# Feed-forward of a two-layer encoder: two parts projected down together, twelve products to a bank

## The chip, the cores and the metric

The kernel runs on one core of one Trainium2 chip. A core has a matrix engine (TensorE, in the profile PE, with PEld for its weight loads), a vector engine (VectorE, DVE), an engine for activations and copies (ScalarE, ACT), a general one (GpSimd, POOL), and DMA queues that SyncE (SP) issues here. The engines run side by side, each through its own list of instructions in order, and wait for one another by semaphores. The metric is the device time of one execution in microseconds; lower is better.

## The reference

Two sequences of 1024 channels, a prompt of 256 tokens and a sample of 512, go through two layers and a last norm. Each layer is a mixer (an mLSTM in the first, attention in a window in the second) and a feed-forward with a convolution of width 3, both with a residual. The change lies in the feed-forward alone:

```python
def conv_ffn(h, w_up, conv_w, conv_b, w_down):
    u = h @ w_up                       # 1024 -> 2 * 2816
    u = lax.conv_general_dilated(u, conv_w[:, None, :], window_strides=(1,), ...) + conv_b
    g = u[..., :D_FF]
    val = u[..., D_FF:]
    return (jax.nn.silu(g) * val) @ w_down   # 2816 -> 1024

x = x + g2 * conv_ffn(h, ffn_w_up[l], ffn_conv_w[l], ffn_conv_b[l], ffn_w_down[l])
```

## The kernel before

**Columns and precision.** Prompt and sample stand side by side as 768 columns. A matrix product in fp32 is made of three in a shorter format: each operand is split into a high and a low half (`whi`, `wlo` for weights, `zh`, `zl` and the like for activations), and high·high, high·low and low·high are added in a PSUM bank. A split is a cast on ACT (L275, the high half) and a subtraction on DVE (L276, the low half). Raw weights come by DMA in pieces of 512 KB (`raw`, 5 buffers); the split weights have 3 buffers each.

**Parts.** `Net.ffn` works through the 2816 channels in `NPART` = 11 parts of 256. For a part p, `up(p)` projects 1024 channels to 256 gates and 256 values, convolves them, and forms silu(gate)·value; `down(p, g)` projects these 256 channels back to 1024 and adds into the residual slab `xt`. Written order: up(0), up(1), down(0), up(2), down(1), and so on to up(10), down(9), down(10). The framework's scheduler makes each engine's list out of this, so pieces of neighbouring steps interleave.

**A projection up.** `pair` (called for i = 0, the gates, and i = 1, the values) replaces eight quarter products by seven, with sums of weights and of activations. A quarter is 12 matmuls of 128x384 (L1350 high·high, L1351 high·low, L1353 low·high). The seven are called B11, B21, B22 and T1 to T4 after the activations that they read, and go to four banks that stay the same: a (B11, then B21), e (T1), b (T2 on top of a copy of B11, then B22), d (T3 on top of a copy of T2, then T4). In the listings with numbers these banks are `ps_4468` (a), `ps_4469` (e), `ps_4470` (b) and `ps_4471` (d). Between them stand copies on ACT: L1399 (a into b, before T2), L1404 (T1 out), L1410 (b into d, before T3), L1421 (T3 out, before T4 may write d), L1363 (a row out); and DVE's L1423 and L1424, which finish the rows. POOL makes the sums of raw weights (L1383, L1386, L1387, L1395). The convolution is L1587 on ACT and L1589, L1590 on DVE; the silu is L1597 on ACT.

**The product.** `product` multiplies gate and value on POOL (L1602, in two halves) and splits the result into a slab `g` (L275 and L276). Slabs are large buffers, 6 in all: 2 for `xt`, 2 for the rows of u, and 2 that `yrow` and `g` take in turn.

**A projection down.** `down` has two halves of weights, and in each 4 blocks of 128 output channels for the sample's 512 columns and the prompt's 256: 16 tiles. A tile is 6 matmuls (L269) into one bank of `pa` (4 banks); then `resid`, one instruction on DVE (L602), adds the bank, scaled, into `xt`. The last part, down(10), goes through ranges of 256 columns and runs the next norm behind them. Its code stays.

Of the kernel before, what the change touches and what calls it, by code (L numbers as in the profile page):

```python
# [12 lines left out]
R = mybir.dt.float32r  # L13
# [3 lines left out]
P = 128  # L17
# [7 lines left out]
RANGES = ((256, 512, 0), (512, 768, 0), PROMPT)  # L25
# [5 lines left out]
TG = T + GAP  # L31
# [3 lines left out]
NPART = FC // 2  # L35
# [45 lines left out]
def col(t):  # L81

    return t + (GAP if t >= 256 else 0)
# [7 lines left out]
class Norm:  # L91
# [31 lines left out]
    held = False  # L123
# [58 lines left out]
class Net:  # L182
# [1389 lines left out]
    def ffn(self, l, xt, pool, last_tile, apply, keep=None):  # L1572
        nc = self.nc
        u0 = U_FFN + l * NPART * 3
        early = self.prepare(u0)
        next(last_tile)

        urows = [self.slab([P, 4, TG]) for _ in range(2)]
        for urow in urows:
            nc.gpsimd.memset(urow[:, :, 256 : 256 + GAP], 0.0)  # L1580

        behind = []

        def conv(u, y, ch):
            cb = self.cst(CB + l * 44 + ch)
            w = lambda tap: self.cst(CW + (l * 44 + ch) * 3 + tap)
            nc.scalar.activation(y, u, AF.Identity, bias=cb, scale=w(1))  # L1587
            stt = nc.vector.scalar_tensor_tensor
            stt(y[:, 1:], u[:, :-1], w(0), y[:, 1:], ALU.mult, ALU.add)  # L1589
            stt(y[:, :-1], u[:, 1:], w(2), y[:, :-1], ALU.mult, ALU.add)  # L1590


        held = []

        def silu(yrow):
            for j in range(2):
                nc.scalar.activation(yrow[:, j], yrow[:, j], AF.Silu)  # L1597

        def product(yrow, g):
            for j in range(2):  # L1600
                y = yrow[:, 2 + j]
                nc.gpsimd.tensor_tensor(y, y, yrow[:, j], ALU.mult)  # L1602
                self.fp_copy_split(g[:, 0, j], g[:, 1, j], y)

        def up(p):
            urow = urows[0] if p == 0 else urows[1]
            fixed = lambda i: self.bank[i][:, :H]
            if p == 0:
                eng = mybir.EngineType
                self.ready(HALVES[0])  # L1610
                with self.tc.manual_schedule(engines={eng.PE, eng.Activation, eng.DVE}):
                    behind[:] = self.head(u0, last_tile, pool, urows, mark, early)
            yrow = self.slab([P, 4, TG])
            g = self.slab([P, 2, 2, TG], R)
            for i in range(2):
                if p:
                    rows = [urow[:, 2 * i + j] for j in range(2)]
                    with ExitStack() as order:
                        for ins in behind[2 * i :] if p == 1 else ():
                            order.enter_context(self.tc.issue_after(ins))  # L1620

                        other = p == i == 1
                        bank = lambda j: self.pa()[:, :H] if j == 1 and other else fixed(j)
                        self.pair(pool, u0 + 3 * p + i, bank, rows, p == 1, held.pop() if held else None)
                for j in range(2):
                    conv(urow[:, 2 * i + j], yrow[:, 2 * i + j], i * FC + 2 * p + j)
                if i == 0:
                    held.append(lambda: silu(yrow))
            if p:
                product(yrow, g)  # L1630
            else:
                gate = held.pop()
                held.append(lambda: (gate(), product(yrow, g)))
            return g

        def mark(t):

            hi, _ = self.quarter(self.B11)
            self.mm(t, hi[0][:, :P], hi[0], True, True)

        def down(p, g):
            ws = (w for _, w in self.halves(u0 + 3 * p + 2))
            chunk = lambda w, i: [t[:, 512 * i : 512 * (i + 1)] for t in w]

            def tile(w, c, rng, more=False):
                s0, s1, _ = rng
                alone = keep is None and p == NPART - 1
                o = (self.ps() if more and (c % 2 or alone) else self.pa())[:, : s1 - s0]
                cs = slice(c % 4 * P, (c % 4 + 1) * P)
                for i in range(2):  # L1650
                    wh, wl = chunk(w, i)
                    gh, gl = (g[:, z, i, col(s0) : col(s0) + s1 - s0] for z in range(2))
                    self.mm(o, wh[:, cs], gh, i == 0, False)
                    self.mm(o, wh[:, cs], gl, False, False)
                    self.mm(o, wl[:, cs], gh, False, i == 1)
                return self.resid(xt, o, l, 40, c, rng)

            if p < NPART - 1:
                for h, w in enumerate(ws):
                    for rng in SAMPLE, PROMPT:  # L1660
                        for c in range(4 * h, 4 * h + 4):
                            tile(w, c, rng, p == NPART - 2)
                return
            ws = list(ws)
            for rng in RANGES:
                final = keep is None and rng is RANGES[-1]
                norm = Norm(
                    self, xt, rng, apply, 3 if final else 4 if keep is None and rng is RANGES[1] else 2, final,
                    wait=0.0 if keep is None or rng is RANGES[-1] else 1.3,
                )  # L1670
                for c in range(KC):
                    done = tile(ws[c // 4], c, rng, keep is None or rng is not RANGES[-1])
                    norm.square(c)
                    if final and c >= KC - 2:
                        self.ends.append(done.ins)
                    if final and c == KC - 1:
                        norm.sums = [norm.sums[i] for i in (1, 2, 0, 3)]
                        norm.begin(1)
                    self.tick(0.65)
                if keep is not None:  # L1680
                    self.save_x(xt, keep, rng)
                self.start(rng, norm.stages())

        prev = None
        for p in range(NPART):
            g = up(p)
            if prev is not None:
                down(*prev)
            prev = (p, g)
        down(*prev)  # L1690


    def run(self):
# [178 lines left out]
```

## Time and profile before

| what | value |
|---|---|
| runs of the kernel | median 1809.89 us of 3, from 1808.83 to 1811.03 |
| the profiled execution | 1808.25 us |
| its span, first to last instruction | 1806.4 us |
| granted clock of TensorE, mean | 0.996 |
| feed-forward of the first layer | about 477 to 1015 us of the span |
| feed-forward of the second layer | about 1260 to 1806 us |

The profile is of one execution. Its rows name a line of the kernel, an engine, an operation and the buffers, written out<-in; "busy" is the time in which an engine works on something, "idle" the time ahead of an instruction, with what ended it behind the arrow. In a timeline the first number is the start, the second the duration. Matmuls overlap: one of 384 columns lasts 0.34 us in the rows while the next starts after some 0.17, so starts tell more than durations. Windows give the busy time of each engine in a stretch of the span.

### The profile page before, as it was taken

The page shows a single profiled execution, that of the slowest core. Times are in us where ns is not written, and L with a number is a line of the kernel's source. Part 1 is how long each engine was busy: PE and PEld are TensorE (multiplying, and loading weights), DVE is VectorE, ACT ScalarE, POOL GpSimd, SP SyncE. Part 2 cuts the span into 40 slices and gives each one's busy share as a digit, 9 for nine tenths or more (in the row PEclk, how much of TensorE's full clock was granted, in tenths as well). Part 3 has the DMA queues.
Part 4 walks back from the last instruction along what each step waited for, and adds up shares of the span by engine and source line. Part 5 has one row for each costly group of instructions (what it writes and reads, how often), then busy time and mean ns, then how long its engine had stood idle before and what let it go on. Part 6 is the DMA issues. An engine that isn't in the chain of part 4 may idle for free.

```text
span 1806.4 us, 28907 instructions
## 1 busy us (share of the span) xinstructions
PE 1773.1 (98%) x11206; PEld 1644.4 (91%) x11206; DVE 1384.8 (77%) x2219; ACT 887.8 (49%) x1789; POOL 488.2 (27%) x397
## 2 busy tenths in 40 slices
PE   7999999999999999999999999999999999999998
PEld 4988888889998999999999999889989999999997
DVE  4876777895799778777777867767998777777877
ACT  4544433444565444444444657665564444444443
POOL 3000000031024333333331313320144333333323
PEclk9999999999999999999999999999999999999999
DMA  9344665656212222222223331234122222222212
GB/s 360 98 140 135 196 207 180 215 180 219 71 59 71 62 67 71 70 71 71 67 64 94 106 93 42 60 92 138 48 82 71 71 71 71 70 70 71 70 36 71
DMA packets 64997, 185.08 MB, mean 102 GB/s; under 512 B 6247, under 2 KB 24839, under 8 KB 64732
## 3 DMA queue, kind: packets, MB, share of 16 engines
q1 hardware_dynamic: 64284, 182.72, 31.3%
q8 instruction: 88, 1.44, 0.3%
q10 hardware_dynamic: 576, 0.52, 0.1%
q14 instruction: 49, 0.40, 0.1%
HBM read 176.77 MB, written 6.44 MB: 101 GB/s over the span
## 4 chain that ended last, share of the span: by engine, by line
PE 87%; DVE 5%; DMA 3%; ACT 3%; issue 1%; POOL 1%; SPq 0%; DVEq 0%; ACTq 0%; POOLq 0%
PE ps L269 28%; PE pa L269 24%; PE ps L1350 11%; PE ps L1351 10%; PE ps L1353 10%; DMA raw<-in_adaln_t_dram 1%; PE pa L1189 1%; DVE junk L538 1%; DMA slab<-in_adaln_w_dram 1%; DVE wlo L276 1%; PE pa L1350 0%; PE pa L1351 0%; PE pa L1353 0%; ACT zh L1301 0%; DMA raw<-in_adaln_w_dram 0%
## 5 line engine op out<-in xcount | busy, mean ns | idle before, releaser
L275 ACT CAST whi<-raw 128x1024 fp32r<-128x1024 f32 (+1 forms) x231 | 241.0, 1045 | 339.0 <-PE pa L269 144.4
L276 DVE TENSOR_TENSOR wlo<-raw,whi 128x1024 fp32r<-128x1024 f32 (+1 forms) x231 | 312.6, 1354 | 119.1 <-ACT whi L275 116.8
L269 PE MATMUL pa<-slab,whi 128*128 128x256 f32 (+1 forms) x1280 | 307.6, 335 | 0.0
L269 PEld LDWEIGHTS pa<-slab,whi 128*128 128x128 f32 x1280 | 222.2, 188 | 21.6 <-DVE slab L602 0.4
L602 DVE SCALAR_TENSOR_TENSOR slab<-pa,mod,slab 128x256 f32<-128x256 f32 (+1 forms) x320 | 187.2, 603 | 62.7 <-PE pa L269 62.6
L269 PE MATMUL pa<-slab,wlo 128*128 128x512 f32 (+1 forms) x640 | 205.7, 334 | 0.0
L269 PE MATMUL ps<-zh,whi 128*128 128x256 f32 (+1 forms) x560 | 188.1, 337 | 0.3 <-ACT zh L948 0.3
L269 PE MATMUL ps<-zl,whi 128*128 128x256 f32 (+1 forms) x560 | 183.6, 330 | 0.5 <-DVE zl L563 0.5
L269 PE MATMUL ps<-zh,wlo 128*128 128x256 f32 (+1 forms) x560 | 181.7, 330 | 0.0
L1350 PE MATMUL ps<-zh,whi 128*128 128x384 f32 x504 | 172.6, 342 | 3.8 <-ACT nt L1421 2.0
L269 PE MATMUL ps<-slab,whi 128*128 128x384 f32 (+2 forms) x704 | 172.0, 329 | 0.9 <-DVE slab L276 0.5
L1351 PE MATMUL ps<-zl,whi 128*128 128x384 f32 x504 | 169.9, 337 | 0.8 <-DVE zl L1307 0.8
L1353 PE MATMUL ps<-zh,wlo 128*128 128x384 f32 x504 | 169.1, 336 | 0.0
L538 DVE CUSTOM_DVE_ANT_0 junk<-raw,crow,cstt 128x1024 f32<-128x1024 f32 x96 | 125.2, 1305 | 25.1 <-DMA raw<-in_adaln_t_dram 24.5
L1386 POOL TENSOR_TENSOR raw<-raw,raw 128x512 f32<-128x512 f32 x40 | 53.8, 1344 | 319.4 <-DVE wlo L276 246.3
L269 PEld LDWEIGHTS pa<-slab,wlo 128*128 128x128 f32 x640 | 120.4, 188 | 13.2 <-DVE wlo L276 0.4
L1602 POOL TENSOR_TENSOR slab<-slab 128x772 f32<-128x772 f32 x44 | 86.5, 1969 | 163.7 <-DVE slab L1590 150.5
L1589 DVE SCALAR_TENSOR_TENSOR slab<-slab,cstt,slab 128x771 f32<-128x771 f32 x88 | 105.4, 1200 | 26.5 <-ACT slab L1587 26.4
L269 PEld LDWEIGHTS ps<-slab,whi 128*128 128x128 f32 x704 | 122.5, 188 | 3.4 <-ACT whi L275 0.9
L269 PEld LDWEIGHTS ps<-zh,whi 128*128 128x128 f32 x560 | 106.8, 191 | 12.8 <-issue 3.5
L269 PEld LDWEIGHTS ps<-zl,whi 128*128 128x128 f32 x560 | 106.8, 191 | 9.5 <-DVE zl L563 0.7
L269 PE MATMUL ps<-slab,wlo 128*128 128x384 f32 (+2 forms) x352 | 114.8, 328 | 0.1
(301 smaller groups left out, 4286.8 us busy)
## 6 DMA issues: line engine op xcount, KB each, us to landing
raw<-in_w_dram SPq DMA_DIRECT2D x208, 512.0 KB, 3.7
raw<-in_adaln_t_dram SPq DMA_DIRECT2D x48, 512.0 KB, 4.2
raw<-in_adaln_w_dram SPq DMA_DIRECT2D x36, 512.0 KB, 4.5
slab<-in_x_dram SPq DMA_DIRECT2D x12, 512.0 KB, 7.2
slab<-in_adaln_w_dram SPq DMA_DIRECT2D x11, 512.0 KB, 9.2
slab<-mrows SPq DMA_DIRECT2D x8, 384.0 KB, 6.3
xs<-slab SPq DMA_DIRECT2D x6, 512.0 KB, 3.6
bt<-brow SPq DMA_DIRECT2D x16, 192.0 KB, 3.1
```

The source lines that it names most:

```text
L269: self.nc.tensor.matmul(out, lhsT, rhs, start=start, stop=stop)
L275: nc.scalar.copy(hi, src)
L276: return nc.vector.tensor_tensor(lo, src, hi.bitcast(F32), ALU.subtract)
L538: nc.vector.tensor_tensor_reduce(out=junk, in0=w, in1=row[:, s], scale=1.0, scalar=self.cst(AB + 48 * l + j), op0=ALU.mult, op1=ALU.add, a ...
L602: return self.nc.vector.scalar_tensor_tensor(x, o, self.mod[l][:, gc + c, q : q + 1], x, ALU.mult, ALU.add)
L1189: nc.tensor.transpose(pp[:, ks], b.t[:, e, ks], self.ident)
L1350: mm(o, wh[:, k], hi[k], start=start and k == 0, stop=False, skip_group_check=True)
L1351: mm(o, wh[:, k], lo[k], start=False, stop=False, skip_group_check=True)
L1353: mm(o, wl[:, k], hi[k], start=False, stop=k == 3, skip_group_check=True)
L1386: tt(q[0], q[2], q[0], ALU.subtract)
L1589: stt(y[:, 1:], u[:, :-1], w(0), y[:, 1:], ALU.mult, ALU.add)
L1602: nc.gpsimd.tensor_tensor(y, y, yrow[:, j], ALU.mult)
```

## The change

`down` takes two parts at once, (0, 1), (2, 3) and so on to (8, 9), and each of its 16 tiles now adds the six matmuls of the first part and the six of the second in one bank before `resid` takes it out. Both parts' first halves of weights are loaded, then both second halves. The order of the steps becomes up(0), up(1), up(2), down(0, 1), up(3), up(4), down(2, 3), to up(10), down(8, 9), down(10). The slabs `g` of two parts now have to live at once with a `yrow`. So `g` is taken only when the product is split, `yrow` only after the first `pair` is written, and the split of an even part from 2 on is held back: it is issued behind the copy L1410 (`fork`) of the next projection's first `pair`, through `behind`. An odd part's product is split at once.

```diff
@@ -1596,11 +1596,21 @@
             for j in range(2):
                 nc.scalar.activation(yrow[:, j], yrow[:, j], AF.Silu)
 
-        def product(yrow, g):
+        gs = {}
+
+        def product(yrow, p, now):
+            def part(j):
+                if not j:
+                    gs[p] = self.slab([P, 2, 2, TG], R)
+                self.fp_copy_split(gs[p][:, 0, j], gs[p][:, 1, j], yrow[:, 2 + j])
+
             for j in range(2):
                 y = yrow[:, 2 + j]
                 nc.gpsimd.tensor_tensor(y, y, yrow[:, j], ALU.mult)
-                self.fp_copy_split(g[:, 0, j], g[:, 1, j], y)
+                if now:
+                    part(j)
+            if not now:
+                held.append(lambda: [part(j) for j in range(2)])
 
         def up(p):
             urow = urows[0] if p == 0 else urows[1]
@@ -1610,8 +1620,7 @@
                 self.ready(HALVES[0])
                 with self.tc.manual_schedule(engines={eng.PE, eng.Activation, eng.DVE}):
                     behind[:] = self.head(u0, last_tile, pool, urows, mark, early)
-            yrow = self.slab([P, 4, TG])
-            g = self.slab([P, 2, 2, TG], R)
+            yrow = None
             for i in range(2):
                 if p:
                     rows = [urow[:, 2 * i + j] for j in range(2)]
@@ -1622,46 +1631,49 @@
                         other = p == i == 1
                         bank = lambda j: self.pa()[:, :H] if j == 1 and other else fixed(j)
                         self.pair(pool, u0 + 3 * p + i, bank, rows, p == 1, held.pop() if held else None)
+                yrow = yrow or self.slab([P, 4, TG])
                 for j in range(2):
                     conv(urow[:, 2 * i + j], yrow[:, 2 * i + j], i * FC + 2 * p + j)
                 if i == 0:
                     held.append(lambda: silu(yrow))
             if p:
-                product(yrow, g)
+                product(yrow, p, p % 2 == 1)
             else:
                 gate = held.pop()
-                held.append(lambda: (gate(), product(yrow, g)))
-            return g
+                held.append(lambda: (gate(), product(yrow, p, True)))
 
         def mark(t):
 
             hi, _ = self.quarter(self.B11)
             self.mm(t, hi[0][:, :P], hi[0], True, True)
 
-        def down(p, g):
-            ws = (w for _, w in self.halves(u0 + 3 * p + 2))
+        def down(parts):
+            of = [self.halves(u0 + 3 * p + 2) for p in parts]
+            g = [gs.pop(p) for p in parts]
             chunk = lambda w, i: [t[:, 512 * i : 512 * (i + 1)] for t in w]
 
-            def tile(w, c, rng, more=False):
+            def tile(ws, c, rng, more=False):
                 s0, s1, _ = rng
-                alone = keep is None and p == NPART - 1
+                alone = keep is None and len(parts) == 1
                 o = (self.ps() if more and (c % 2 or alone) else self.pa())[:, : s1 - s0]
                 cs = slice(c % 4 * P, (c % 4 + 1) * P)
-                for i in range(2):
+                steps = [(w, x, i) for w, x in zip(ws, g) for i in range(2)]
+                for w, x, i in steps:
                     wh, wl = chunk(w, i)
-                    gh, gl = (g[:, z, i, col(s0) : col(s0) + s1 - s0] for z in range(2))
-                    self.mm(o, wh[:, cs], gh, i == 0, False)
+                    gh, gl = (x[:, z, i, col(s0) : col(s0) + s1 - s0] for z in range(2))
+                    self.mm(o, wh[:, cs], gh, w is ws[0] and i == 0, False)
                     self.mm(o, wh[:, cs], gl, False, False)
-                    self.mm(o, wl[:, cs], gh, False, i == 1)
+                    self.mm(o, wl[:, cs], gh, False, w is ws[-1] and i == 1)
                 return self.resid(xt, o, l, 40, c, rng)
 
-            if p < NPART - 1:
-                for h, w in enumerate(ws):
+            if len(parts) == 2:
+                for h in range(2):
+                    ws = [next(x)[1] for x in of]
                     for rng in SAMPLE, PROMPT:
                         for c in range(4 * h, 4 * h + 4):
-                            tile(w, c, rng, p == NPART - 2)
+                            tile(ws, c, rng, parts[1] == NPART - 2)
                 return
-            ws = list(ws)
+            ws = [w for _, w in of[0]]
             for rng in RANGES:
                 final = keep is None and rng is RANGES[-1]
                 norm = Norm(
@@ -1669,7 +1681,7 @@
                     wait=0.0 if keep is None or rng is RANGES[-1] else 1.3,
                 )
                 for c in range(KC):
-                    done = tile(ws[c // 4], c, rng, keep is None or rng is not RANGES[-1])
+                    done = tile(ws[c // 4 : c // 4 + 1], c, rng, keep is None or rng is not RANGES[-1])
                     norm.square(c)
                     if final and c >= KC - 2:
                         self.ends.append(done.ins)
@@ -1681,13 +1693,12 @@
                     self.save_x(xt, keep, rng)
                 self.start(rng, norm.stages())
 
-        prev = None
         for p in range(NPART):
-            g = up(p)
-            if prev is not None:
-                down(*prev)
-            prev = (p, g)
-        down(*prev)
+            up(p)
+            if p > 1 and p % 2 == 0:
+                down((p - 2, p - 1))
+        held.pop()()
+        down((p,))
 
 
     def run(self):
```

Lines below the change stand 7 to 11 lines further down than in the profile of before.

**TensorE where up(1) ends and up(2) begins, first layer.** Of before; the first two rows are the end of T1 of up(2), `pa` are banks of down(0), and the last row is the first of T3 of up(1).

```order
L1351 MATMUL ps_4469<-zl,s1h_5870 128x384
L1353 MATMUL ps_4469<-zh,s1l_5871 128x384
L269 MATMUL pa_5723<-slab_5493,whi_5719 128x512 x2
L269 MATMUL pa_5731<-slab_5493,whi_5719 128x512 x2
L269 MATMUL pa_5739<-slab_5493,whi_5719 128x512 x2
L269 MATMUL pa_5723<-slab_5493,wlo_5720 128x512
L269 MATMUL pa_5723<-slab_5493,whi_5719 128x512
L269 MATMUL pa_5731<-slab_5493,wlo_5720 128x512
L269 MATMUL pa_5731<-slab_5493,whi_5719 128x512
L269 MATMUL pa_5739<-slab_5493,wlo_5720 128x512
L269 MATMUL pa_5739<-slab_5493,whi_5719 128x512
L1350 MATMUL ps_4471<-zh,whi_5628 128x384
```

Of the change, the same place:

```order
L1351 MATMUL ps_4469<-zl,s1h_5728 128x384
L1353 MATMUL ps_4469<-zh,s1l_5729 128x384
L1350 MATMUL ps_4468<-yh,whi_5722 128x384
L1351 MATMUL ps_4468<-yl,whi_5722 128x384
L1353 MATMUL ps_4468<-yh,wlo_5723 128x384
L1350 MATMUL ps_4468<-yh,whi_5722 128x384
```

The twelve products of down(0), six of them on high weights ahead of the first on low ones, are gone from here; B11 of up(2) follows T1 at once, and reads its low weights in its third product.

**ScalarE at the same place.** Of before, from the silu of up(1) on:

```order
L1597 ACTIVATE slab_5506<-slab_5506 128x772 x2
L1421 COPY nt_5675<-ps_4471 128x384
L1404 COPY nt_5896<-ps_4469 128x384
L275 CAST whi_5789<-raw_5787 128x1024
L1587 ACTIVATE slab_5506<-slab_5043,cstt 128x772
L275 CAST whi_5864<-raw_5861 128x1024
L1363 COPY slab_5043<-ps_4471 128x128
L1363 COPY slab_5043<-ps_4471 128x256
L1587 ACTIVATE slab_5506<-slab_5043,cstt 128x772
L1399 COPY ps_4470<-ps_4468 128x384
```

Of the change:

```order
L1597 ACTIVATE slab_5604<-slab_5604 128x772 x2
L1421 COPY nt_5674<-ps_4471 128x384
L1404 COPY nt_5754<-ps_4469 128x384
L275 CAST whi_5745<-raw_5719 128x1024
L1587 ACTIVATE slab_5604<-slab_5043,cstt 128x772
L1399 COPY ps_4470<-ps_4468 128x384
```

The copy L1399 that fills bank b for T2 of up(2) stands behind one cast and one convolution step in place of two of each and two copies out.

**TensorE from T2 to T3 in a projection of a later part, first layer.** Of before, from the end of T2 (bank `ps_4470`) to the start of T3 (`ps_4471`):

```order
L1351 MATMUL ps_4470<-zl,whi_7219 128x384
L1353 MATMUL ps_4470<-zh,wlo_7220 128x384
L1353 MATMUL ps_4468<-yh,wlo_7197 128x384
L1350 MATMUL ps_4468<-yh,whi_7196 128x384
L1351 MATMUL ps_4468<-yl,whi_7196 128x384
L1353 MATMUL ps_4468<-yh,wlo_7197 128x384
L1350 MATMUL ps_4471<-zh,whi_7223 128x384
L1351 MATMUL ps_4471<-zl,whi_7223 128x384
```

Of the change, in a projection of the same region, from the end of T2 on; eight more rows of B21 (`ps_4468`) follow on the last before T3 starts:

```order
L1351 MATMUL ps_4470<-zl,whi_7154 128x384
L1353 MATMUL ps_4470<-zh,wlo_7155 128x384
L1350 MATMUL ps_4468<-yh,whi_7131 128x384
L1351 MATMUL ps_4468<-yl,whi_7131 128x384
L1353 MATMUL ps_4468<-yh,wlo_7132 128x384
L1350 MATMUL ps_4468<-yh,whi_7131 128x384
```

Before, four products of B21 stand between T2 and T3, the others ahead of them among T2's; in the change all twelve of B21 stand between.

## The prediction

> **What bounds the kernel now.** I read the page first (busy time of each engine, then the chain that ended last), then the stretches of the two feed-forwards by engine, then the waits of TensorE in them, row by row.
>
> ```profile
> PE 1773.1 (98%) x11206; PEld 1644.4 (91%) x11206; DVE 1384.8 (77%) x2219; ACT 887.8 (49%) x1789; POOL 488.2 (27%) x397
> PE 87%; DVE 5%; DMA 3%; ACT 3%; issue 1%; POOL 1%; SPq 0%; DVEq 0%; ACTq 0%; POOLq 0%
> ```
>
> TensorE (PE) is the bound. VectorE (DVE) is busy for three quarters of the span, but only 5% of the chain is DVE. What the change saves is DVE work, so the question is where in the feed-forward PE waits at all. The windows below have the columns core, PE, PEld, DVE, ACT, POOL, granted clock, DMA share, GB/s.
>
> ```profile
> core 0: us, PE busy (x) PEld busy (x) DVE busy (x) ACT busy (x) POOL busy (x), PEclk, DMA share, GB/s
> 477.00:560.00 83.00, 79.06 (x441) 74.90 (x441) 78.66 (x104) 50.91 (x94) 23.59 (x15) 1.00 0.23 74
> 560.00:640.00 80.00, 80.00 (x462) 75.99 (x462) 64.61 (x75) 37.21 (x57) 32.42 (x19) 1.00 0.19 60
> ...
> 696.07:742.45 46.38, 46.38 (x266) 43.83 (x265) 35.68 (x41) 21.52 (x35) 16.49 (x10) 1.00 0.23 69
> 742.45:788.78 46.33, 46.33 (x265) 43.93 (x265) 35.51 (x42) 21.51 (x35) 17.30 (x10) 1.00 0.22 69
> ...
> 1260.00:1340.00 80.00, 76.08 (x425) 71.95 (x424) 75.99 (x101) 50.06 (x92) 23.32 (x15) 1.00 0.22 70
> ```
>
> Two regimes. From about 560 us on, one part of 256 channels takes 46.35 us and PE has no idle time in it; DVE is at 35.6 of 46.35. In the first 83 us (and from 1260 in the second layer) DVE is at 95% and PE idles 3.9 us in each layer.
>
> The steady part isn't quite free of loss. PE's rows at the first product of T3, with the copy on ScalarE (ACT) that fills its bank:
>
> ```profile
> 769.42 0.33 PE L1353 MATMUL ps<-yh,wlo 128*128 128x384 f32 x1
> 769.59 0.43 PE L1350 MATMUL ps<-zh,whi 128*128 128x384 f32 x1
> 769.86 0.34 PE L1351 MATMUL ps<-zl,whi 128*128 128x384 f32 x1
> 770.03 0.34 PE L1350 MATMUL ps<-bq,whi 128*128 128x384 f32 x1
> ...
> 784.17 0.34 PE L1353 MATMUL ps<-yh,wlo 128*128 128x384 f32 x1
> 784.36 0.44 PE L1350 MATMUL ps<-zh,whi 128*128 128x384 f32 x1
> 784.64 0.33 PE L1351 MATMUL ps<-zl,whi 128*128 128x384 f32 x1
> ...
> 768.10 1.05 ACT L275 CAST whi<-raw 128x1024 fp32r<-128x1024 f32 x1 [8.14 <-PE pa L269]
> 769.05 0.47 ACT L1410 COPY ps<-ps 128x384 f32<-128x384 f32 x1
> 783.85 0.46 ACT L1410 COPY ps<-ps 128x384 f32<-128x384 f32 x1 [0.83 <-PE ps L1353]
> ```
>
> A product of 384 columns starts every 0.17 to 0.175 us; behind the product at 769.59 the next starts after 0.27, and likewise at 784.36. So each of a part's two T3 loses **0.1 us** because the copy L1410 ends only as PE gets there. The real waits are at the start of each layer's feed-forward, and one small one later:
>
> ```profile
> 544.28 0.34 PE L1353 MATMUL pa<-zh,s1l 128*128 128x384 f32 x1
> 545.59 0.44 PE L1350 MATMUL ps<-zh,whi 128*128 128x384 f32 x1 [0.97 <-ACT nt L1421]
> 545.87 0.34 PE L1351 MATMUL ps<-zl,whi 128*128 128x384 f32 x1
> ...
> 548.66 0.44 PE L1350 MATMUL ps<-zh,whi 128*128 128x384 f32 x1 [0.71 <-ACT ps L1399]
> ...
> 552.74 0.45 PE L1353 MATMUL ps<-zh,s1l 128*128 128x384 f32 x1 [1.38 <-DVE s1l L276]
> ...
> 645.31 0.44 PE L1350 MATMUL ps<-zh,whi 128*128 128x384 f32 x1 [0.20 <-ACT ps L1410]
> ```
>
> An idle time of 0.97 costs 545.59 − 544.28 − 0.175 = 1.135, and 0.1 more behind it: 0.27 over the idle shown. The four lose 1.24, 0.98, 1.65 and 0.47 us.
>
> **The change part by part.**
>
> *DVE.* Each joined pair adds 16 banks into x instead of 32: five pairs in each of two layers, so 160 additions go, half of them of either width.
>
> ```profile
> L602 DVE SCALAR_TENSOR_TENSOR slab<-pa,mod,slab 128x512 f32<-128x512 f32 x152 | 111.0, 743 | 25.3 <-PE pa L269 25.3
> L602 DVE SCALAR_TENSOR_TENSOR slab<-pa,mod,slab 128x256 f32<-128x256 f32 x168 | 76.7, 477 | 37.4 <-PE pa L269 37.2
> ```
>
> That is 80 × 0.743 + 80 × 0.477 = **97.6 us of DVE time**, some 5 us of each part's 35.6. No steady wait of PE is for DVE, so it is worth **0** on the path. PE's products are the same in number and shape, and so are the casts, splits, POOL sums and DMAs: 0.
>
> *T3 behind B21.* In the order of before, T3 stands four to six products behind T2 (0.7 to 1.05 us) in parts 4 to 10; in the change all twelve of B21 (2.1 us) stand between, in every pair of parts 3 to 10. The copy needs 0.47 and, at worst, the rest of a 1.05 cast ahead of it, so it is in time. What goes: 7 parts × 2 T3 × 2 layers × 0.095 = **−2.7 us**. Nothing is late next there; should the cast still be in the way, it is 0.
>
> *up(2) right behind up(1).* Here the change adds waits. Before, PE went from T1 of up(2) into down(0):
>
> ```profile
> 554.41 0.34 PE L1353 MATMUL ps<-zh,s1l 128*128 128x384 f32 x1
> 554.59 1.54 PE L269 MATMUL pa<-slab,whi 128*128 128x512 f32 x6
> 555.97 0.44 PE L269 MATMUL pa<-slab,wlo 128*128 128x512 f32 x1
> ...
> 553.54 2.31 DVE L276 TENSOR_TENSOR wlo<-raw,whi 128x1024 fp32r<-128x1024 f32 x1
> ...
> 559.12 1.01 DVE L1590 SCALAR_TENSOR_TENSOR slab<-slab,cstt,slab 128x771 f32<-128x771 f32 x1
> 561.94 0.55 DVE L1423 TENSOR_TENSOR slab<-ps,nt 128x384 f32<-128x384 f32 x1
> ...
> 560.98 0.46 ACT L1421 COPY nt<-ps 128x384 f32<-128x384 f32 x1
> 561.34 0.48 ACT L1404 COPY nt<-ps 128x384 f32<-128x384 f32 x1
> 561.70 1.06 ACT L275 CAST whi<-raw 128x1024 fp32r<-128x1024 f32 x1
> ```
>
> The low weights at 553.54 are ready at 555.85, and before covered this with six products on the high weights. In the change DVE has its rows in the same order up to L1423, so the same slot makes the low weights of up(2)'s B11; but B11 wants them at its third product, 554.59 + 2 × 0.175 = 554.94. PE waits until 555.97: 1.03, and 0.1 behind it, **+1.13**. Everything on PE stands behind it, so B11 ends at 557.8, T3 of up(1) at 559.9, B22 at 562.0. T4 needs L1421, which (behind a silu that waits for L1590) ended at 561.44: no wait. T4 ends at 564.1. T2 of up(2) needs L1399, queued on ACT behind the cast at 561.70 and a convolution step (about 0.93 each): it ends near 564.05, too late by the 0.1 of a close arrival, **+0.1**. Then up(2)'s second T3 stands two products behind T2, as one does before at 645.31: the same 0.47, in another place, 0.
>
> Per layer +1.23, so **+2.5** over both. Bounds: 0 if POOL leaves that split alone (1.21 instead of 2.31, row 743.58 below, would end it at 554.75); 3.9 per layer if all of up(1)'s three waits come again at up(2). I take the worked value, nearest to the rows of that very place.
>
> *The held split.* The even part's split waits behind L1410 of the next projection, on ACT and DVE, where nothing but that projection's T1 cast and T3 follow it; the joined down comes 50 us later. 0, and with that cover gone a cast and a split, 2.3 us.
>
> *Joined down, weights through three buffers.* The second half of the second part takes the buffer of the first half of the first; by the order, 6 narrow products, 18 wide ones of 0.23 and 3 of T1 lie between, about 5.4 us. The next pair's T2 weights get about 3.9 us. A cast and a split, alone or beside a POOL product:
>
> ```profile
> 743.58 1.21 DVE L276 TENSOR_TENSOR wlo<-raw,whi 128x1024 fp32r<-128x1024 f32 x1
> ...
> 748.04 1.95 DVE L276 TENSOR_TENSOR wlo<-raw,whi 128x1024 fp32r<-128x1024 f32 x1
> ...
> 747.04 1.87 POOL L1602 TENSOR_TENSOR slab<-slab 128x772 f32<-128x772 f32 x1 [5.40 <-DVE slab L1590]
> ```
>
> 1.05 + 1.21 = 2.3, beside POOL 3.0: hidden, 0. The split at 748.04 lost 0.74 while POOL's product ran on to 748.91. [...]
>
> *Tail.* down of part 10 keeps its code, and its split lies beneath the down ahead of it: 0.
>
> *Sum.* 1808.25 (the profiled execution, span 1806.4) − 2.7 + 2.5 = 1808.05. The median of the runs, 1809.89, lies 1.64 above the profiled one: **1809.7**.
>
> **The rivals.**
> 1. *Faster*: the T3 losses go, up(2) doesn't wait (freed DVE clears its queue first), the 0.47 goes in both layers: −2.7 − 0.9 = −3.6, so 1806.3. At most 0.01 us for each of 160 bank openings saved (rows show starts to a hundredth, and none is seen) would add −1.6: 1804.7. Against: down(0)'s additions stood behind L1423 in DVE's queue, so nothing is freed before it.
> 2. *Slower*: up(2) runs into the crowded start as up(1) did. Price up to 3.9 per layer, +7.7 − 2.7, so 1814.9, or 1817.6 with the T3 losses kept. It decides if DVE's queue is still behind at T2 and T4 of up(2), past 566 us. For: DVE at 95% until 560. Against: 81% after it.
> 3. *Slower*: the weights in the joined down miss. One cast and split unhidden per join, 2.3 us × 10, gives 1833. Against: 3.9 us of cover.
> 4. *Slower*: between pairs back to back, L1399 on ACT must come within T1's 2.1 us. The same join stands inside each part before, without loss; 27 of them at 0.2 would be +5.4: 1815.
> 5. *It doesn't do what it says*: pieces of twelve broken up. The order shows twelve to a bank; 1809.9.
>
> **How the numbers follow.** The forecast, with its parts between half and double, 0.60; rival 1 0.15, rival 2 0.12, rival 3 0.03, rival 4 0.07, rival 5 0.03. 0.2% (3.6 us) is about what a measurement of this kernel can tell from no change. Forecast and rival 5 are within it: 0.63; faster 0.15; rivals 2 to 4 slower: 0.22. The range reaches from the far end of rival 1, cut at 1805, to the end of rival 2, 1817.5; outside it are rival 3, and some of 1, 2 and 4.
>
> **What would show it.** The two L602 groups with 160 instances in place of 320, and DVE near 1287 us. T3 rows in steady parts 0.175 us apart. A wait of about 1.0 us for `wlo` L276 at B11 of up(2), once per layer. Two projections and half a joined down take 46.3 us each. I'd be wrong if PE showed idle time inside a joined down, or behind each pair at T2.

## The result, and the profile after

| kernel | time, median of its runs | the kernel before beside it | ratio, 95% interval |
|---|---|---|---|
| the change | 1819.82 us (1818.69 to 1820.51) | 1809.36 us | 1.0063 (1.0051 to 1.0076) |

The change is **slower by 0.63%**, some 11 us. The forecast was no change, 1809.7 us with a range up to 1817.5: the time lies outside it. The profiled execution took 1820.38 us, its span 1818.6 against 1806.4. These are the page's lines of the change that answer to those of before:

```profile
PE 1778.7 (98%) x11206; PEld 1652.3 (91%) x11206; DVE 1299.2 (71%) x2059; ACT 888.6 (49%) x1789; POOL 480.6 (26%) x397
PE 81%; DVE 8%; ACT 3%; POOL 3%; DMA 2%; issue 2%; SPq 0%; POOLq 0%; DVEq 0%; ACTq 0%
```

VectorE lost the 160 instructions and 86 us of busy time, as the change says. But its share of the chain went from 5% to 8%, and POOL's from 1% to 3%: less work, and more of it in the way. The stretches by engine (columns as before) and the two groups of L602:

```profile
core 0: us, PE busy (x) PEld busy (x) DVE busy (x) ACT busy (x) POOL busy (x), PEclk, DMA share, GB/s
477.00:560.00 83.00, 79.27 (x440) 76.07 (x439) 78.94 (x102) 49.45 (x91) 28.48 (x18) 0.98 0.20 64
560.00:600.00 40.00, 36.36 (x189) 34.16 (x188) 32.84 (x30) 24.44 (x39) 14.57 (x9) 0.96 0.25 79
...
696.07:742.45 46.38, 46.38 (x281) 44.00 (x281) 25.90 (x31) 16.80 (x26) 12.51 (x9) 1.00 0.18 54
...
1340.00:1400.00 60.00, 56.61 (x305) 53.48 (x304) 47.95 (x46) 30.40 (x49) 23.83 (x13) 0.94 0.21 65
```

```profile
L602 DVE SCALAR_TENSOR_TENSOR slab<-pa,mod,slab 128x512 f32<-128x512 f32 x72 | 53.7, 746 | 70.2 <-PE pa L269 70.2
L602 DVE SCALAR_TENSOR_TENSOR slab<-pa,mod,slab 128x256 f32<-128x256 f32 x88 | 42.4, 483 | 65.6 <-PE pa L269 65.5
```

PE idles 3.6 us in 560 to 600, where before it had none, and the granted clock is below 1.00 in both early stretches. What PE waited for in the change from 530 to 600 us, and then from 600 to 1000 us (total us, times, longest):

```profile
PE ps L1350 <- ACT nt L1421: 4.9, 2, 2.6
PE ps L1353 <- DVE wlo L276: 0.8, 1, 0.8
PE ps L1353 <- DVE s1l L276: 0.6, 1, 0.6
PE ps L1350 <- ACT ps L1410: 0.2, 1, 0.2
```

```profile
PE ps L1350 <- ACT ps L1399: 1.7, 4, 0.4
```

Two places, then. At the start, PE waits for L1421 twice, 2.28 and 2.61 us, where before it waited 0.97 us once. In the later parts it waits 0.42 us for L1399 four times; the same view of before has no such row there. The second layer repeats both. With 0.27 us on top of each wait and the time lost to slower matmuls behind the long ones (2.6 us in the first layer, 3.8 in the second, from the spacing of PE's rows), the start loses 10.5 us per layer against 4.3 before (the four losses that the prediction lists). So the start gives 2 × 6.2 = 12.4 us, the eight waits for L1399 give 8 × 0.69 = 5.5, and the T3 losses that went give back some 2.5. That is 15.4, while the two feed-forwards are 13.6 us longer from their first to their last rows (the rest of the span is 1.4 us shorter): 1.8 us of this account are small differences that I can't place.

### The profile page after: what moved, and what is told of

Read it like the earlier page. It is cut to its first block, busy times and chain, and to the rows that moved or that the text cites. A ratio compares the mean times of both kernels' runs of the same rounds, so it can differ in the third digit from the quotient of the medians.

```text
span 1818.6 us, 28813 instructions
## 1 busy us (share of the span) xinstructions
PE 1778.7 (98%) x11206; PEld 1652.3 (91%) x11206; DVE 1299.2 (71%) x2059; ACT 888.6 (49%) x1789; POOL 480.6 (26%) x397
## 4 chain that ended last, share of the span: by engine, by line
PE 81%; DVE 8%; ACT 3%; POOL 3%; DMA 2%; issue 2%; SPq 0%; POOLq 0%; DVEq 0%; ACTq 0%
PE ps L269 30%; PE pa L269 23%; PE ps L1350 8%; PE ps L1351 8%; PE ps L1353 8%; DVE wlo L276 2%; PE pa L1189 1%; ACT whi L275 1%; DMA slab<-in_adaln_w_dram 1%; DVE slab L1589 1%; DMA raw<-in_adaln_t_dram 1%; POOL raw L1395 1%; POOL raw L1386 1%; DVE s1l L276 1%; DVE junk L538 1%
## 5 line engine op out<-in xcount | busy, mean ns | idle before, releaser
L276 DVE TENSOR_TENSOR wlo<-raw,whi 128x1024 fp32r<-128x1024 f32 (+1 forms) x231 | 324.5, 1412 | 86.0 <-ACT whi L275 84.8
L269 PE MATMUL pa<-slab,whi 128*128 128x256 f32 (+1 forms) x1216 | 287.5, 334 | 0.0
L269 PEld LDWEIGHTS pa<-slab,whi 128*128 128x128 f32 x1216 | 206.0, 188 | 22.8
L269 PE MATMUL pa<-slab,wlo 128*128 128x256 f32 (+1 forms) x608 | 195.9, 333 | 0.0
L602 DVE SCALAR_TENSOR_TENSOR slab<-pa,mod,slab 128x256 f32<-128x256 f32 (+1 forms) x160 | 96.1, 602 | 135.8 <-PE pa L269 135.7
L269 PE MATMUL ps<-slab,whi 128*128 128x384 f32 (+2 forms) x768 | 187.6, 330 | 0.9 <-DVE slab L276 0.5
L1589 DVE SCALAR_TENSOR_TENSOR slab<-slab,cstt,slab 128x771 f32<-128x771 f32 x88 | 118.6, 1349 | 34.5 <-ACT slab L1587 34.2
L269 PEld LDWEIGHTS ps<-slab,whi 128*128 128x128 f32 x768 | 133.5, 188 | 5.0 <-ACT whi L275 0.9
L1383 POOL TENSOR_TENSOR raw<-raw 128x512 f32<-128x512 f32 x40 | 69.1, 1727 | 205.7 <-DMA raw<-in_w_dram 204.7
L1587 ACT ACTIVATE slab<-slab,cstt 128x772 f32<-128x772 f32 x88 | 91.1, 1036 | 58.2 <-DVE slab L1423 56.2
```

The lines of the kernel that those rows point to most:

```text
L269: self.nc.tensor.matmul(out, lhsT, rhs, start=start, stop=stop)
L276: return nc.vector.tensor_tensor(lo, src, hi.bitcast(F32), ALU.subtract)
L602: return self.nc.vector.scalar_tensor_tensor(x, o, self.mod[l][:, gc + c, q : q + 1], x, ALU.mult, ALU.add)
```

## The experiments

Ratios are to runs of the kernel before on the same chip. Kernels of different tables below ran on different chips.

| experiment | median, us | before, us | ratio, 95% interval |
|---|---|---|---|
| first two parts alone | 1808.99 | 1808.03 | 1.0009 (1.0000 to 1.0017) |
| copy ahead of the cast | 1816.48 | 1808.03 | 1.0048 (1.0035 to 1.0061) |
| filler ahead of T4 | 1825.40 | 1808.03 | 1.0099 (1.0084 to 1.0115) |
| sums left out | 1813.05 | 1808.03 | 1.0028 (1.0016 to 1.0039) |

### The first two parts projected down alone

```diff
-            if p > 1 and p % 2 == 0:
+            if p in (1, 2):
+                down((p - 1,))
+            elif p and p % 2 == 0:
                 down((p - 2, p - 1))
```

Left out here are the lines that let `down` take a single part ahead of the last one.

> The change, but parts 0 and 1 are projected down alone, each where the kernel before has it (down(0) behind up(1), down(1) behind up(2)); parts (2,3) to (8,9) stay joined. Theory 'start': most of the loss lies where up(2) follows up(1) at once. The two waits of 2.3 and 2.6 us for L1421 and the slow matmuls behind them go, the three waits of before (0.97, 0.71, 1.38 us) come back in each layer: 14 us less at the start against 8 more, so about 1811 to 1814 us, and what is left over before is the waits for L1399 in the later parts. Rival 'joining': the joined down itself costs the time (its weights, its slabs); then four of five joined pairs keep four fifths of the loss, about 1817 us, with the start as in the change.

1808.99 us, and at the start the three waits of before are back within 0.02 us (0.97, 0.70, 1.36). PE's waits from 530 to 600 us:

```profile
PE ps L1353 <- DVE s1l L276: 1.4, 1, 1.4
PE ps L1350 <- ACT nt L1421: 1.0, 1, 1.0
PE ps L1350 <- ACT ps L1399: 0.7, 1, 0.7
```

With four of five pairs still joined the time is nearly that of before, so **the joined down is not what costs; the order at the start is**. It came 2 us under what I expected. What is left in its trace is eight waits for L1399, 5.5 us, against the T3 losses gone.

### POOL's sums for part 2 left out

```diff
-        tt = nc.gpsimd.tensor_tensor
+        tt = (lambda *a: None) if bare else nc.gpsimd.tensor_tensor
```

`bare` is true for the gates of part 2 alone, in both layers (the call that says so is left out here). The kernel then computes other numbers for these gates; all other instructions stay.

> The change without POOL's four sums of raw weights for the gates of part 2 (the gates of this part are then of other numbers). The order of all other instructions is the same on every engine. Theory 'port': these sums run beside VectorE's convolutions and splits of part 1, which take twice as long for it, the silus come late, and PE waits 2.3 and 2.6 us for L1421. Without them VectorE's rows there take 0.95, 1.01 and 0.68 again, the first wait is about 1 us and the second under 0.6, no slow matmuls follow, T2 of up(1) and T1 of up(2) wait again as before (0.7 and 1.4): 4 to 5 us less in each layer, about 1810 to 1812 us. Rival 'cover': it is the missing products of down(0) alone that expose the waits; then they stay over 2 us and the time is 1818 to 1820 us.

1813.05 us, 1 us above what I expected, and a ratio 0.0035 under that of the change, about 6 us; the two feed-forwards are 8.0 us shorter in the profiles. The place is this one, in the timeline of the change (start, duration): three instructions of DVE, POOL's sums of up(2)'s weights beside them, and what follows on DVE, ACT and PE.

```profile
555.19 2.04 DVE L276 TENSOR_TENSOR slab<-slab,slab 128x772 fp32r<-128x772 f32 x1
557.15 2.05 DVE L1589 SCALAR_TENSOR_TENSOR slab<-slab,cstt,slab 128x771 f32<-128x771 f32 x1
559.13 1.77 DVE L276 TENSOR_TENSOR s1l<-raw,s1h 128x512 fp32r<-128x512 f32 x1
560.82 1.01 DVE L1590 SCALAR_TENSOR_TENSOR slab<-slab,cstt,slab 128x771 f32<-128x771 f32 x1
...
554.46 1.94 POOL L1386 TENSOR_TENSOR raw<-raw,raw 128x512 f32<-128x512 f32 x1 [2.75 <-issue]
556.48 1.90 POOL L1387 TENSOR_TENSOR raw<-raw 128x512 f32<-128x512 f32 x1
558.35 2.01 POOL L1395 TENSOR_TENSOR raw<-raw,raw 128x512 f32<-128x512 f32 x1
...
561.93 0.85 ACT L1597 ACTIVATE slab<-slab 128x772 f32<-128x772 f32 x1 [5.78 <-DVE slab L1590]
562.68 0.46 ACT L1421 COPY nt<-ps 128x384 f32<-128x384 f32 x1
...
563.19 0.69 PE L1350 MATMUL ps<-zh,whi 128*128 128x384 f32 x1 [2.61 <-ACT nt L1421]
```

And with the sums left out, the same four instructions of DVE in the same order:

```profile
555.71 0.95 DVE L276 TENSOR_TENSOR slab<-slab,slab 128x772 fp32r<-128x772 f32 x1
556.58 1.01 DVE L1589 SCALAR_TENSOR_TENSOR slab<-slab,cstt,slab 128x771 f32<-128x771 f32 x1
557.51 0.68 DVE L276 TENSOR_TENSOR s1l<-raw,s1h 128x512 fp32r<-128x512 f32 x1
558.11 1.01 DVE L1590 SCALAR_TENSOR_TENSOR slab<-slab,cstt,slab 128x771 f32<-128x771 f32 x1
```

Beside POOL, three instructions last 5.86 us; without it 2.64. So L1590, the silu behind it, and L1421 behind the silu are 3 us late, and PE finds T4's bank not drained. Without the sums the wait of 2.61 is gone and the one of 2.28 is 0.97 again. PE's waits from 530 to 600 us without them:

```profile
PE ps L1353 <- DVE s1l L276: 1.4, 1, 1.4
PE ps L1353 <- DVE wlo L276: 1.3, 1, 1.3
PE ps L1350 <- ACT nt L1421: 1.0, 1, 1.0
PE ps L1350 <- ACT ps L1399: 0.9, 2, 0.7
PE ps L1350 <- ACT ps L1410: 0.2, 1, 0.2
```

The wait of 1.3 us for low weights, one in each layer, is what is left here in the main over the first two parts alone: it is not of these sums. Where POOL had the four sums of up(2)'s gates before, and the first of them in the change:

```profile
543.62 2.25 POOL L1383 TENSOR_TENSOR raw<-raw 128x512 f32<-128x512 f32 x1
567.79 1.29 POOL L1386 TENSOR_TENSOR raw<-raw,raw 128x512 f32<-128x512 f32 x1 [13.02 <-issue]
569.16 1.89 POOL L1387 TENSOR_TENSOR raw<-raw 128x512 f32<-128x512 f32 x1
571.02 2.02 POOL L1395 TENSOR_TENSOR raw<-raw,raw 128x512 f32<-128x512 f32 x1
```

```profile
531.67 2.01 POOL L1383 TENSOR_TENSOR raw<-raw 128x512 f32<-128x512 f32 x1
```

Before, three of them run behind the crowded stretch, and L1383 behind the first product on POOL. The change has L1383 ahead of that product; of the four it alone runs before the wait of 2.28, so that wait hangs on it. Beside the sums (1.94, 1.90 and 2.01 us on POOL) the three instructions of DVE took 2.04, 2.05 and 1.77 us, and without them 0.95, 1.01 and 0.68. What makes them longer isn't shown.

### Control: the same sums left out of the kernel before

The same edit, in the kernel before.

> Control for the fifth experiment: the kernel before, without POOL's four sums of raw weights for the gates of part 2 (those gates are of other numbers); everything else keeps its order. Before, down(0) stands between up(1) and up(2), and these sums run when VectorE is past its crowd. Theory 'port and place': they cost nothing there, so the time is that of the kernel before, within 2 us. Rival: POOL's sums cost some 4 us a layer wherever they stand; then it is 1800 us.

| experiment | median, us | before, us | ratio, 95% interval |
|---|---|---|---|
| before, sums left out | 1804.91 | 1808.55 | 0.9982 (0.9973 to 0.9991) |
| copy ahead but in up(1) | 1805.87 | 1808.55 | 0.9984 (0.9975 to 0.9993) |

Between the two: 3.6 us less by the medians, and 2.3 us less over the two feed-forwards by the profiles (the wait of 0.71 for L1399 goes). The sums cost something before as well, where I had expected the same time within 2 us. Of the 8.0 us of the experiment above, **5.7 us are thus of their place in the change** by the profiles. By the ratios, 0.0035 against 0.0018, it is about 3 us, and the intervals are as wide as that. So the rows show that the place of the sums costs time; whether 3 or 6 us is not settled.

### The copy L1399 ahead of the cast

```diff
-        wb = self.split(rb)
         e, b = bank(1), bank(2)
-        nc.scalar.copy(b, fork)
+        if rest:
+            wb = self.split(rb)
+        first = nc.scalar.copy(b, fork)
+        if not rest:
+            with self.tc.issue_after(first.ins):
+                wb = self.split(rb)
```

> The change, with the copy L1399 (a into b, ahead of T2) queued on ScalarE in front of the cast of the weights for T3 and T4, except in up(1). Theory 'join': L1399 is late by 0.42 us at T2 eight times, since it stands behind a cast that waits for POOL's sum L1395. Each costs 0.58 and 0.1 behind it: 8 x 0.69 = 5.5 us less, about 1814 us, and no wait of PE for L1399 in the later parts. Rival: the copy waits for VectorE's L1423 or for B11 anyway; then the waits stay and the time is 1819 to 1820 us.

Of the change, where PE waits for L1399, the timeline of POOL, ACT and PE:

```profile
671.59 2.02 POOL L1395 TENSOR_TENSOR raw<-raw,raw 128x512 f32<-128x512 f32 x1
...
673.63 1.05 ACT L275 CAST whi<-raw 128x1024 fp32r<-128x1024 f32 x1 [0.92 <-POOL raw L1395]
674.60 0.53 ACT L1363 COPY slab<-ps 128x128 f32<-128x128 f32 x2
675.01 0.49 ACT L1399 COPY ps<-ps 128x384 f32<-128x384 f32 x1
...
674.80 0.34 PE L1353 MATMUL ps<-zh,s1l 128*128 128x384 f32 x1
675.55 0.44 PE L1350 MATMUL ps<-zh,whi 128*128 128x384 f32 x1 [0.42 <-ACT ps L1399]
```

The copy itself could go some 2 us before (the last product of B11, whose bank it copies, starts at 672.72 us, and ACT idles 0.92 us ahead of the cast); it stands in ACT's queue behind a cast that waits for POOL. The time, 1816.48 us, lies between what I expected and the rival's. With the copy first, no wait for L1399 is left from 600 to 1000 us, and the two feed-forwards are 4.7 us shorter in the profiles (5.5 expected). By the medians the ratio falls by 0.0015, 2.7 us, but the two intervals overlap. The last experiment below makes the same edit on top of the first two parts alone: there the ratio falls by 0.0025, 4.5 us, and the intervals lie apart.

### Filler where PE waits for L1421

```diff
+            t = self.pa()[:, :H]
+            hi, _ = self.quarter(self.B22)
+            with self.tc.issue_after(tail.ins):
+                for _ in range(fill):
+                    self.mm(t, hi[0][:, :P], hi[0], True, True)
         self.quarters(d, part(wb, 1), self.T4, False)
```

> The change plus eight matmuls of 128x384 in each projection of up(1), behind B22, into a bank that nothing reads. They add work only where PE waits for L1421. Theory 'clock': behind an idle time of 2.28 us or more PE runs at 1.83 times the usual spacing for about 3 us; with 1.4 us of filler the idle times fall to 0.9 to 1.3 us, the spacing of 0.32 us vanishes, and T4 starts where it did: 1.5 to 1.8 us less at four places, about 1813 us. Rival: the slow matmuls are not for the idle time (power, or weights that come slowly): they stay and the time is 1820 us or a little more.

The edit is shown without the call, which gives 8 as `fill` for up(1) and 0 elsewhere. A miss as a measurement: the filler also changed the order of PE in up(2), and a wait of 2.8 us for L1399 appeared there in both layers. 1825.40 us says nothing of the clock. So it was made smaller, with 3 as `fill`, which keeps the order but for two products. In the change the granted clock is 0.50 in four stretches, one at the end of each wait for L1421 (the last section has them). If the idle time brings them, some should go when it is shorter; I expected 1814 to 1819 us:

> The change plus three matmuls of 128x384 (0.52 us) in each projection of up(1) where PE waits for L1421; the rest keeps its order. The idle times there become about 1.76 and 2.09 us. [...] Rival: the half clock has nothing to do with the idle time: four or more stretches stay.

| experiment | median, us | before, us | ratio, 95% interval |
|---|---|---|---|
| three fillers | 1818.96 | 1807.66 | 1.0063 (1.0047 to 1.0078) |
| six to a bank | 1828.57 | 1807.66 | 1.0114 (1.0100 to 1.0128) |
| split at once | 1824.00 | 1807.66 | 1.0088 (1.0075 to 1.0102) |
| both mended | 1806.15 | 1807.66 | 0.9993 (0.9985 to 1.0002) |

First the change, then the one with three fillers, 530 to 600 us:

```profile
530.00:600.00 70.00, 63.50 (x333) 60.62 (x332) 62.80 (x53) 43.52 (x70) 31.54 (x17) 0.95 0.25 78
```

```profile
530.00:600.00 70.00, 62.33 (x337) 58.64 (x337) 62.28 (x53) 42.80 (x68) 32.51 (x17) 1.00 0.25 77
...
PE ps L1350 <- ACT nt L1421: 3.9, 2, 2.1
PE ps L1353 <- DVE wlo L276: 2.6, 2, 1.3
PE ps L1353 <- DVE s1l L276: 0.6, 1, 0.6
```

The granted clock is 1.00 throughout, so the slow matmuls are gone, and yet the time is that of the change. PE now comes earlier to the low weights of up(2) and waits there: 2.6 us in place of 0.8. Both waits for L1421 end where they did, 55.0 and 72.9 us behind the feed-forward's first product (55.0 and 72.8 in the change). **At the start DVE's queue sets the pace** (62 of 70 us busy), and what PE loses to its clock is mostly time in which it would have waited.

### Six products to a bank in the change's order

```diff
-                steps = [(w, x, i) for w, x in zip(ws, g) for i in range(2)]
-                for w, x, i in steps:
+                for w, x in zip(ws, g):
+                    o = (self.ps() if more and (c % 2 or alone) else self.pa())[:, : s1 - s0]
+                    for i in range(2):
...
+                    done = self.resid(xt, o, l, 40, c, rng)
```

> The change's order of parts, but six products to a bank: each tile of a joined down takes one bank for the first part and another for the second, and L602 has its 320 instances back. Theory 'order': it is where the projections stand that costs, not the banks; the waits for L1421 at the start and for L1399 later stay, the 98 us of VectorE come back beside PE's work, and the time is that of the change, 1817 to 1820 us. Rival 'bank': twelve to a bank is itself dear (a bank is held twice as long) or itself worth something; then it leaves that range, by 3 us or more.

1828.57 us: my theory fell. The 160 additions are back, and the change's order with them is 0.0051 worse, about 9 us. Over the two feed-forwards it is 7.2 us in the profiles, and most of it lies in PE's waits for L1399 and L1410. From 600 to 1000 us they are (beside 1.7 in all in the change):

```profile
PE ps L1350 <- ACT ps L1399: 3.3, 4, 1.0
PE ps L1350 <- ACT ps L1410: 0.8, 4, 0.2
```

Twelve to a bank is thus worth 7 to 9 us in an order in which two projections follow one another; by which path the additions delay those copies isn't shown. In the order of before, with a down between any two, PE has one wait of 0.2 us from 600 to 1000 us, so there the additions could delay little.

### The even part's split at once

```diff
-                product(yrow, p, p % 2 == 1)
+                product(yrow, p, p < NPART - 1)
```

> The change, but an even part's product is split at once, as an odd part's is, and not behind L1410 of the next projection. Only these splits move on ScalarE and VectorE; PE's order is the same. The slab they write is free only after the joined down's last product, so in four pairs of a layer ScalarE and VectorE stand still behind that split. Theory: the hold is needed; L1399 and the casts behind the split come later by its wait, up to 1 or 2 us at each of eight joins, 1820 to 1835 us. Rival: the hold itself costs (it puts two casts ahead of the next T1 and T3); then it is 1 to 3 us faster than the change.

1824.00 us, a ratio 0.0025 over that of the change (the intervals just meet), 2.8 us longer over the two feed-forwards in the profiles: the rival falls. In four pairs of each layer (at 632.52, 725.65, 818.62 and 911.74 us in the first) PE loses 0.2 and then 0.1 us at T2, where the change loses nothing: L1399 stands behind the two casts of the split. That is 2.4 us in all, so the hold is worth having.

### Both causes mended

The first experiment's order of parts, and the copy first in every projection; then the same, with up(1) left as it was.

> Parts 0 and 1 projected down alone as in the first experiment, and the copy L1399 ahead of the cast in every projection, up(1) too. If start and join are the two causes and add: 1809.0 - 5.5 for eight waits at T2 - about 1 us in each layer, since up(1)'s L1421 no longer stands behind that cast (a wait of 0.97 us there) = 1801.5 to 1804 us, under the kernel before. If the two causes overlap or the copy's move makes the weights for T3 late: 1806 us or more.

> As both mended (parts 0 and 1 alone, L1399 ahead of the cast), but up(1) keeps its cast first, as in the kernel before. In both mended, the waits at up(1) only changed their places (1.67 for the copy and 1.77 for the split in place of 0.97, 0.70 and 1.36), so this should have the waits of before there and the same time as both mended: 1804 to 1807 us, 1 to 3 us under the kernel before (the losses at T3 gone, 2.7 us). If it is 1808 us or more, moving the copy in up(1) was worth something after all; if it is under 1803 us, it cost.

Both mended take 1806.15 us, above the 1801.5 to 1804 that I expected, and the ratio, 0.9993 (0.9985 to 1.0002), doesn't tell it from the kernel before. In up(1) the copy's move only changed which wait it is: 1.67 us for the copy and 1.77 for the split of T1's weights, in place of 0.97, 0.70 and 1.36. Its expected gain of 1 us in each layer didn't come. With up(1) left alone the kernel takes 1805.87 us, ratio 0.9984 (0.9975 to 0.9993): **2.7 us faster than before, and faster than the change**. It keeps four joined pairs per layer. Its waits at the start are those of before; the T3 losses and the waits for L1399 later are gone. New in both is one wait of 0.56 us in each layer for low weights (at 665.51 us in the first layer of the last run).

## Why the prediction was wrong, by its own steps

- **DVE.** The count was right: 160 instructions. The two groups of L602 lost 91.6 us, DVE in all 86, forecast 97.6, since other instructions grew longer. "Worth 0 on the path" holds beside the order of before only. In the change's own order the additions would cost 7 to 9 us.
- **T3 behind B21**, −2.7 us: right. The products at T3 in parts 4 to 10 stand 0.17 us apart in the change.
- **up(2) right behind up(1)**, +2.5 us: this is the step that failed. I put before's own times into the new order: the low weights at 555.85, L1421 at 561.44, both because "DVE has its rows in the same order". It does, but the rows change in length. The order on POOL had moved too, and I had put its sums at 0 because they are "the same in number and shape". The same DVE instructions took 3.2 us longer beside the sums; L1421 ended at 563.14, and PE waited 2.61 us at a T4 for which I had written "no wait". The wait that I did forecast, 1.03 for the low weights of B11, didn't come in the change: their split took 1.21 instead of 2.31 and was ready. That was my lower bound's reason, and the cost went elsewhere. It came in the run with three fillers, 1.32 us, once PE, without its slow products, got there earlier. The measured size of this step, with up(1)'s own waits in it, is 12.2 us (the two feed-forwards of the change against those of the first two parts alone, in the profiles; by the ratios it is 10), not 2.5.
- **up(1)'s own waits** I took as unchanged. The first grew from 0.97 to 2.28, since the sum L1383 moved ahead on POOL.
- **The second T3 of up(2)**, 0.47 in another place: right (0.36 and 0.11 at 587 us).
- **Joined down, weights through three buffers**: right. PE doesn't idle in a joined down, and rival 3 falls.
- **The held split**, 0: no wait of PE in the change is put down to it, and with the split at once the kernel was slower.
- **Rivals.** Rival 2, "up(2) runs into the crowded start", is what happened, at some 12 us instead of 7.7, and by POOL's sums beside DVE, which it didn't name. Rival 4, L1399 late between pairs, happened too: not 27 joins at 0.2, but 8 at 0.69, and not by T4's end but by a cast that stood ahead of it and waited for POOL. I gave the two 0.12 and 0.07, as if each came alone. They came together, and together they lie above the range.

What stays open: how much the sums' place costs, 3 or 6 us, and how that divides between the two long waits and the low weights, since each hides some of the next; and 1.8 us of the account above.

## What to carry to other kernels

When a change takes a block of matrix work out from between two others, ask what else was late and hidden beneath it, and follow the order of *every* engine there, POOL too: a short instruction on one engine can stretch those of another (here 0.95 us became 2.04 beside a sum on POOL), so durations from the old profile hold only for the old neighbours. A copy that releases the bound engine should not stand in a queue behind an instruction that waits for a third engine (here 0.42 us, eight times). In a crowded stretch single waits don't add: taking some of one away can lengthen the next (with three fillers 0.8 us for the low weights became 2.6).

## What the runs showed of the hardware

**At the end of each long wait of the change, PE ran at half its clock for some us.** In the change, behind the idle time of 2.28 us that ended at 545.39, products started 0.32 us apart for 3.2 us, and then 0.17 again. The granted clock of these two stretches:

```profile
545.90:549.00 3.10, 3.10 (x11) 3.10 (x10) 3.10 (x5) 1.33 (x3) 0.00 (x0) 0.50 0.51 169
549.20:552.00 2.80, 2.54 (x15) 2.22 (x13) 2.80 (x3) 2.20 (x4) 1.87 (x1) 1.00 0.60 187
```

At the two starts of the change the granted clock is 0.50 in four stretches, and in each of them products start 0.32 us apart:

| idle time that ended, us | its length, us | granted clock 0.50, us | length, us |
|---|---|---|---|
| 545.39 | 2.28 | 545.81 to 549.22 | 3.41 |
| 563.19 | 2.61 | 562.88 to 566.29 | 3.41 |
| 1334.28 | 2.28 | 1334.29 to 1337.70 | 3.41 |
| 1352.07 | 2.63 | 1351.36 to 1358.18 | 6.82 |

Before, PE's longest wait at the starts is 1.38 us, and the granted clock is 1.00 from 477 to 1015 and from 1260 to 1790 us. With three fillers the two waits for L1421 in the first layer are 3.9 us, the longer one 2.1, and the granted clock is 1.00 from 530 to 600 us. The length of a wait is not all of it: with six to a bank the four waits for L1421 come to 9.8 us, the longest 2.6, as in the change, but the mean granted clock is 0.996 against 0.993. The four stretches of the change alone, 17.1 us at 0.50, would make it 0.995 there, so not all of them came. What else decides it isn't shown.
